# MLP up-projection of a two-layer encoder: the first k-chunk of five of eleven gate/value pairs as a seven-product unit, the gate turned at once and the gate-value product on VectorE

## The chip, the cores and the metric

The kernel runs on one core of one Trainium2 chip. The metric is device time in microseconds (us) of one execution, the median of three runs. Engines: TensorE (PE; its weight loads PEld), VectorE (DVE), ScalarE (ACT), GpSimd (POOL) and SyncE (SP), which issues the weight transfers.

## The reference

Input is x, 256 positions by 2048 features in float32. Two layers: grouped-query attention in the first, dilated sliding-window attention in the second, each followed by the gated MLP to which the change belongs:

```python
def conv_ffn(h, w_up, conv_w, conv_b, w_down):
    u = h @ w_up                       # 2048 -> 2 x 5632
    u = lax.conv_general_dilated(u, conv_w[:, None, :], (1,), ((1, 1),), ...) + conv_b   # depthwise, width 3
    gate, val = jnp.split(u, 2, axis=-1)
    return (jax.nn.silu(gate) * val) @ w_down

h = h + conv_ffn(rms_norm(h, ffn_norm[i]), w_up[i], conv_w[i], conv_b[i], w_down[i])
```

## The kernel before

**Products.** Every float32 product is made of three matmuls on operands split in two: `xh*wh + xh*wl + xl*wh`. A weight chunk of 512 rows by 512 columns comes in two `raw` tiles of 128 x 1024. ScalarE rounds `raw` to `wh` (line 139), VectorE forms `wl = raw - wh` (line 140); of each there are four buffers (`NHL`), and each pair (`wh`, `wl`) feeds 12 matmuls of 128 x 512. `feed` does one chunk (k-chunk `kg`, four k-tiles, two position blocks m): 24 matmuls for one column block. Both calls are recorded AHEAD of their place by a priority, so they stand early on their engines' queues. A scheduler lays the rest out in each engine's queue; every engine runs its queue in order.

**The seven-product unit.** `fast_unit` (lines 159 to 184) takes one k-chunk for two column blocks and does the 2 x 2 block product (two position blocks, two halves of the chunk, two column blocks) with seven products instead of eight: four sums of weight quarters on VectorE (line 173), seven pairs `wh`/`wl` (lines 174, 175), each feeding 6 matmuls: 42 for what two feeds do in 48. It needs sums of the left operand as well (`combined`), and four more PSUM sums (q = 1, 5, 6, 7), which `fold` adds to the others at the end. Before the change it is used in the down-projection and in one output projection only. There the weight sums go to three spare tiles.

**The MLP** (`ffn`). Up-projection: eleven pairs p of a gate block and a value block of 512 columns, p = 0 to 5 (half 0), then the down-projection over these, then p = 6 to 10 (half 1) and the rest of the down-projection. Per block four feeds. When a block's sums are complete they are evacuated with the norm's scale (`stg`, ScalarE), turned position-wise (`turned`: two VectorE transposes, 16 POOL copies into a tile `u`, of which three rotate), convolved (`conv`: ScalarE's centre tap and bias, VectorE's two outer taps, four 256-wide pieces each), silu on the gate `cg`, the product `cv = cg * cv`, and split into the left operands of the down-projection (`act_split`; for k-chunks 1 and 2 `combined`). These steps are Python generators: `start` queues one, and `step`, called between the matmuls of the feeds, advances the first in the list, so their place among the matmuls comes from the number of yields. `gate_gen` of pair p also does `product` of pair p-1; `value_gen` of pair p also does the convolution of its own gate and the split of pair p-1. Before the change the product of a pair is done on POOL, except for the last of each half, and the gate's turn waits for it (`issue_after`).

**Around.** `bias_lines` (lines 1118 to 1139) prepares bias lines of layer 1 beside the up-projection of layer 0. Its transfer of `oc` and its cast `oh` on POOL use slots of the operand store, tiles a0 to a11 (`pair_slot(kt)` is tile kt/2). In layer 0 a0 to a7 hold the operands of the attention output projection until it ends. The last 512 columns of the MLP's input are transposed late (`late_transpose`, n = 3): seven POOL copies `wide` (line 374), then `xh`, while p = 0 already runs over k-chunks 0 to 2.

Of the kernel before, what the change touches and what calls it, by code (L numbers as in the profile page):

```python
# [1 line left out]

# [11 lines left out]
P = 128  # L14
# [16 lines left out]
def tile_encoder(ctx: ExitStack, tc: tile.TileContext, x, xT, w_a, w_ao, q_gain, k_gain, w_b, w_bo,  # L31
# [25 lines left out]
    def nm(s):  # L57
        uid[0] += 1
        return f"{s}_{uid[0]}"
# [92 lines left out]
    def project(w, n, lhs, kgs, by_m=False):  # L152
        accs = new_acc()
        for i, kg in enumerate(kgs):
            end = i == len(kgs) - 1
            feed(accs, lhs, kg, w[n, kg], i == 0, end, by_m and end)
        return accs

    def fast_unit(acc, pick, wap0, wap1, begun, end, spot):
        def load(wap, i):  # L160
            r = raw_tile()
            nc.sync.dma_start(r.rearrange("p a c -> p (a c)"), wap[:, i * 1024:(i + 1) * 1024])
            return r

        b11, b21, b22, b12 = load(wap0, 0), load(wap0, 1), load(wap1, 1), load(wap1, 0)
        t1, t2, t4 = (spot(i) for i in range(3))
        sums = {3: (t1, b11, b12), 5: (b12, b12, b22), 7: (t2, t1, b22), 6: (t4, t2, b21)}
        for i, (q, r) in enumerate(((1, b11), (2, b21), (3, b22), (5, t1), (7, b12), (6, t2), (4, t4))):
            wh = spool.tile([P, 2, 512], F32R, tag="wh", name=nm("wh"), bufs=NHL)
            wl = spool.tile([P, 2, 512], F32R, tag="wl", name=nm("wl"), bufs=NHL)  # L170
            with tc.high_priority(offset=AHEAD):
                if q in sums:
                    nc.vector.tensor_tensor(*sums[q], ALU.add)
                nc.scalar.activation(wh, r, AF.Copy)  # L174
                nc.vector.tensor_tensor(wl, r, wh.bitcast(F32), ALU.subtract)  # L175
            xh, xl = pick[q]
            for j in range(2):
                st = q not in begun and j == 0
                sp = q in end and j == 1
                nc.tensor.matmul(acc[q], xh[:, j], wh[:, j], start=st, stop=False)  # L180
                nc.tensor.matmul(acc[q], xh[:, j], wl[:, j], start=False, stop=False)  # L181
                nc.tensor.matmul(acc[q], xl[:, j], wh[:, j], start=False, stop=sp)  # L182
            begun.add(q)
            step(i % 2 == 0)

# [299 lines left out]
    def ffn(l, hT, ss_in, cw, g_next, last, side=None):  # L485
        with tc.tile_pool(name=nm("fpool"), bufs=1) as fp:
# [82 lines left out]
            def product(value, eng=nc.gpsimd):  # L569
                n, u, cv, cg, made, _, _ = value  # L570
                yield from conv((n, u, cv))
                made.append(eng.tensor_tensor(cv, cg, cv, ALU.mult).ins)  # L572
# [12 lines left out]

            def act_split(value):
                slots, k0 = value[5:]
                cv = value[2]
                if k0 // 4 in fast:
                    slots[-1 - k0 // 4], *parts = combined(cv, k0)  # L590
                    if hf == 1:
                        plain_too(k0, 20 + 2 * fast.index(k0 // 4), *parts)
                    ready.add(k0 // 4)
                    yield
                    return
                for j in range(4):
                    hi, lo = slots[k0 + j]
                    tc.keep_in_program_order(nc.scalar.activation(hi, cv[:, j, :], AF.Copy))
                    nc.vector.tensor_tensor(lo, cv[:, j, :], hi.bitcast(F32), ALU.subtract)
                    if j == 1:  # L600
                        yield
                ready.add(k0 // 4)
# [25 lines left out]

            def flush(value):
                yield  # L630
                yield from product(value, nc.vector)
                ready.add("u")
                yield
                yield
                yield from act_split(value)

            def next_u():
                us.append(us.pop(0))
                return us[0]

            kgs = list(range(4))
            ready = set()
            for hf, (p0, p1) in enumerate(HALVES):
# [4 lines left out]
                last_value = None  # L648
                for p in range(p0, p1):
                    k0 = 4 * (p - p0)  # L650
                    slots.update(new_slots(range(k0, k0 + 4)))
                    cg = fp.tile([P, 4, NT], F32, tag="cg", name=nm("cg"))
                    cv = fp.tile([P, 4, NT], F32, tag="cv", name=nm("cv"))
                    gate, value = (p, next_u(), cg), (NPAIR + p, next_u(), cv, cg, [], slots, k0)

                    def gate_done(accs, gate=gate, last_value=last_value):
                        start(gate_gen(accs, gate, last_value))

                    if p == 0:
# [84 lines left out]

                np_ = p1 - p0
                wd = w_down[l][:, p0:p1]
                extra[0] = fp, ["raw2"]
# [368 lines left out]
    scr = dpool.tile([24, 1024], F32, name="scr")  # L1116

    def bias_lines():
        oc, oh, ln = (pair_slot(kt, [P, 1024], dt, t) for kt, t, dt in ((18, "oc", F32), (20, "oh", F32R), (22, "ln", F32)))
        nc.gpsimd.dma_start(oc, onehot)  # L1120
        rb = small.tile([P, 24], F32, name="rb", bufs=1)
        nc.gpsimd.memset(rb, 0.0)
        nc.gpsimd.memset(rb[32:33, :], -1e30)
        nc.gpsimd.dma_start(rb[:32, :], rel_bias)
        nc.gpsimd.tensor_copy(oh, oc)
# [317 lines left out]
```

## Time and profile before

| | |
|---|---|
| median of three runs | 2239.16 us (2238.94 to 2239.56) |
| the profiled execution: its time, its span | 2238.11 us, 2236.3 us |
| granted clock of TensorE | 0.999 |
| weight transfers (queue q1) | 57.2% of the 16 DMA engines' span, 429.05 MB |
| pairs of half 0, layer 0 | p = 1 from about 301 to 344.6 us, then every 43.5 us |
| pairs of half 1, layer 0 | p = 6 from 645 us, p = 10 to 862.7 us |

A row of a group reads: line, engine, operation, output<-inputs, shapes, count | busy us, mean ns of one | idle time of the engine just before, and who ended it. A row of a timeline reads: start, length, engine, line, operation. Starts and lengths overlap a little, since an engine begins an operation while the one before drains.

### The profile page before, as it was taken

The numbers are of one execution on the slowest core, as the hardware profiler recorded it, in microseconds if no ns is written. First come the engines' busy times: TensorE is split into PE (matmuls) and PEld (weight loads), VectorE is DVE, ScalarE is ACT, GpSimd is POOL, SyncE is SP. The second block draws the span as 40 slices with busy tenths as digits, with TensorE's granted clock in tenths as the row PEclk, the third lists the DMA queues.
The fourth block names the chain that finished last, engine by engine and source line by source line (L and its number), as shares of the span: only waits on it lengthen the run. The fifth ranks groups of instructions, "written<-read, shape, count | busy, mean of one in ns | idle before, by whom it ended". The sixth has DMA issues, their size and how long they took to land.

```text
span 2236.3 us, 28736 instructions
## 1 busy us (share of the span) xinstructions
PE 2221.9 (99%) x10005; PEld 1842.6 (82%) x10005; DVE 1720.0 (77%) x2211; ACT 1321.5 (59%) x1858; POOL 782.3 (35%) x1035
## 2 busy tenths in 40 slices
PE   9999999999999999999999999999999999999998
PEld 7888888888888888888888888888888888888887
DVE  6877667778876787968886878587777798677787
ACT  7676655666455666665454556566665655465664
POOL 2343255752006563040053006003756500256611
PEclk9999999999999999999999999999999999999999
DMA  8565656555665565565556555556556555655653
GB/s 303 193 217 183 220 184 200 192 191 191 203 207 194 192 196 191 197 189 197 189 185 200 177 192 173 200 183 216 194 183 205 184 199 199 210 193 187 217 194 142
DMA packets 126178, 439.58 MB, mean 197 GB/s; under 512 B 14408, under 2 KB 18248, under 8 KB 126032
## 3 DMA queue, kind: packets, MB, share of 16 engines
q1 hardware_dynamic: 123056, 429.05, 57.2%
q0 software_dynamic: 2688, 8.39, 1.5%
q8 instruction: 78, 1.28, 0.2%
q14 instruction: 68, 0.56, 0.1%
q10 hardware_dynamic: 288, 0.30, 0.0%
HBM read 432.34 MB, written 5.34 MB: 196 GB/s over the span
## 4 chain that ended last, share of the span: by engine, by line
PE 53%; DVE 2%; DMA 1%; POOL 1%; issue 0%; ACT 0%; POOLq 0%; DVEq 0%; ACTq 0%
PE acc L128 16%; PE acc L129 16%; PE acc L127 16%; DVE wl L140 1%; DMA raw<-in_w_b_dram 1%; PE ps L181 1%; PE ps L182 1%; PE ps L180 1%; DVE tT L379 1%; PE acc L181 0%; PE acc L182 0%; PE acc L180 0%; POOL wide L391 0%; PE ps L1286 0%; PE ps L332 0%
## 5 line engine op out<-in xcount | busy, mean ns | idle before, releaser
L140 DVE TENSOR_TENSOR wl<-raw,wh 128x1024 fp32r<-128x1024 f32 (+1 forms) x748 | 936.0, 1257 | 351.7 <-ACT wh L139 345.5
L139 ACT ACTIVATE wh<-raw 128x1024 fp32r<-128x1024 f32 (+1 forms) x748 | 783.3, 1050 | 630.5 <-PE acc L129 552.5
L128 PE MATMUL acc<-wl,xh 128*128 128x512 f32 x2176 | 848.1, 390 | 2.2 <-DVE wl L140 2.2
L127 PE MATMUL acc<-wh,xh 128*128 128x512 f32 x2176 | 848.5, 390 | 0.5 <-ACT wh L139 0.5
L129 PE MATMUL acc<-wh,xh 128*128 128x512 f32 x2176 | 846.8, 389 | 0.0
L555 POOL COPY u<-quad 32x256 f32<-32x256 f32 x672 | 480.6, 715 | 326.3 <-DVE quad L370 300.0
L128 PEld LDWEIGHTS acc<-wl,xh 128*128 128x128 f32 x2176 | 408.7, 188 | 88.3 <-DVE wl L140 5.7
L129 PEld LDWEIGHTS acc<-wh,xh 128*128 128x128 f32 x2176 | 408.5, 188 | 84.9
L127 PEld LDWEIGHTS acc<-wh,xh 128*128 128x128 f32 x2176 | 408.6, 188 | 84.5 <-ACT wh L139 1.1
L127 PE MATMUL acc<-wh,a 128*128 128x512 f32 x720 | 280.9, 390 | 0.0
L128 PE MATMUL acc<-wl,a 128*128 128x512 f32 x720 | 280.3, 389 | 0.0
L129 PE MATMUL acc<-wh,a 128*128 128x512 f32 x720 | 280.0, 389 | 0.0
L129 PEld LDWEIGHTS acc<-wh,a 128*128 128x128 f32 x720 | 135.1, 188 | 28.1 <-DVE a L321 0.2
L128 PEld LDWEIGHTS acc<-wl,a 128*128 128x128 f32 x720 | 135.2, 188 | 27.8 <-DVE wl L140 0.4
L127 PEld LDWEIGHTS acc<-wh,a 128*128 128x128 f32 x720 | 135.2, 188 | 27.7
L374 POOL COPY wide<-quad 32x256 f32<-32x256 f32 x133 | 89.6, 674 | 169.3 <-DVE quad L370 159.8
L391 POOL COPY wide<-quad 32x256 f32<-32x256 f32 x88 | 53.1, 603 | 234.6 <-DVE quad L370 167.5
L482 ACT ACTIVATE stg<-acc,rstd 128x512 f32<-128x512 f32 x122 | 82.8, 684 | 32.4 <-PE acc L129 32.4
L174 ACT ACTIVATE wh<-raw 128x1024 fp32r<-128x1024 f32 x56 | 59.5, 1063 | 66.4 <-PE acc L129 59.7
L572 POOL TENSOR_TENSOR cv<-cg,cv 128x1024 f32<-128x1024 f32 x18 | 58.2, 3231 | 105.3 <-DVE cv L542 105.3
L542 DVE SCALAR_TENSOR_TENSOR cg<-u,cw,cg 128x256 f32<-128x256 f32 x176 | 82.3, 511 | 4.5 <-ACT cg L534 4.5
L525 POOL MEMSET u<- 128x4 f32 x12 | 1.0, 106 | 241.3 <-DVE wl L175 221.0
(284 smaller groups left out, 2008.4 us busy)
## 6 DMA issues: line engine op xcount, KB each, us to landing
raw<-in_w_up_dram SPq DMA_DIRECT2D x352, 512.0 KB, 4.5
raw<-in_w_down_dram SPq DMA_DIRECT2D x176, 512.0 KB, 4.5
raw<-in_w_b_dram SPq DMA_DIRECT2D x144, 512.0 KB, 4.3
raw<-in_w_bo_dram SPq DMA_DIRECT2D x48, 512.0 KB, 4.1
raw<-in_w_a_dram SPq DMA_DIRECT2D x40, 512.0 KB, 4.7
raw<-in_w_ao_dram SPq DMA_DIRECT2D x32, 512.0 KB, 4.3
raw<-in_w_a_dram SPq DMA_DIRECT2D x16, 256.0 KB, 6.1
there<-quad POOLq DMA_DIRECT2D x6, 512.0 KB, 3.6
```

Of the source, the lines that this page charges most:

```text
L127: nc.tensor.matmul(accs[m], xh, wh[:, j, :], start=st, stop=False)
L128: nc.tensor.matmul(accs[m], xh, wl[:, j, :], start=False, stop=False)
L129: nc.tensor.matmul(accs[m], xl, wh[:, j, :], start=False, stop=sp)
L139: nc.scalar.activation(wh[:, c], r[:, c], AF.Copy)
L140: nc.vector.tensor_tensor(wl[:, c], r[:, c], wh[:, c].bitcast(F32), ALU.subtract)
L174: nc.scalar.activation(wh, r, AF.Copy)
L374: nc.gpsimd.tensor_copy(o[32 * c:32 * c + 32, :, 32 * q:32 * q + 32], quad[32 * q:32 * q + 32, c])
L391: nc.gpsimd.tensor_copy(dst, src)
L482: nc.scalar.activation(o[:, m, :], accs[m], AF.Copy, scale=rstd[:, m:m + 1])
L542: nc.vector.scalar_tensor_tensor(cj, halves(flat[:, j, o:o + NT])[:, ::-1], tap(n, j, i), cj, ALU.mult, ALU.add)
L555: nc.gpsimd.tensor_copy(o, src)
L572: made.append(eng.tensor_tensor(cv, cg, cv, ALU.mult).ins)
```

## The change

`UP` names p = 1, 4, 6, 7 and 10. For these `up_pair` replaces two `project` calls: three feeds of the gate block (k-chunks 1 to 3), the unit over k-chunk 0 for both blocks, then three feeds of the value block. The gate's sums are folded after the unit, on VectorE, the value's at the end. `sums` makes the left operands' sums once per half. The weight sums are written in place in the `raw` tiles. The product always runs on VectorE, the gate is turned before it, the silu of a gate in `UP` comes two steps later, the two extra `raw` buffers serve the up-projection too, operand slots are taken only when written, and `bias_lines` moves to slots 14, 16 and 18.

```diff
+UP = 1, 4, 6, 7, 10
+UP_ORDER = (1, 0), (2, 0), (3, 0), (0, None), (1, 1), (2, 1), (3, 1)
...
-        t1, t2, t4 = (spot(i) for i in range(3))
+        t1, t2, t4 = (b11, b22, b21) if spot is None else (spot(i) for i in range(3))
...
             def gate_gen(accs, blk, value):
                 s = evac_scaled(fp, accs, rstd, 1)
                 yield
-                if value is None:
-                    turned(s, blk[1])
-                    return
-                yield from product(value)
-                with tc.issue_after(value[4].pop()):
-                    turned(s, blk[1])
+                turned(s, blk[1])
+                if value is not None:
+                    yield
+                    yield from product(value)
...
-                made.append(eng.tensor_tensor(cv, cg, cv, ALU.mult).ins)
+                nc.vector.tensor_tensor(cv, cg, cv, ALU.mult)
...
-                for _ in range(1 if last else 4):
+                for _ in range(3 if gate[0] in UP else 1 if last else 4):
...
+            def sums(kg, at, r, st):
+                hts = [hT[4 * kg + j][:2] for j in range(4)]
+                for j, (hi, lo) in enumerate(hts):
+                    nc.vector.tensor_tensor(r[:, j], hi.bitcast(F32), lo.bitcast(F32), ALU.add)
+                    if j == 1:
+                        yield
...
+                for o, x, y in ((0, a21, a22), (2, a21, a11), (1, a11, st[:, 0]), (3, a12, st[:, 1])):
+                    nc.vector.tensor_tensor(st[:, o], x, y, ALU.subtract)
+                yield
+                own = [pair_slot(at + 2 * i, [P, 4, 2, P], F32R, "s") for i in range(2)]
+                split_in_order(*own, st)
...
+            def up_pair(p, order, gate_done):
+                (a2, a4), (a3, a8) = new_acc(), new_acc()
...
+                    if side is None:
+                        acc.update({q: ps_tile() for q in (1, 5, 6, 7)})
...
+                        fast_unit(acc, picks[kg], *(w_up[l][n, kg] for n in ns), begun, end, None)
+                    else:
...
+                        feed(sides[side], hT, kg, w_up[l][ns[side], kg], not begun.issuperset(mine),
+                             not later & {side, None}, begun=[m for m in range(2) if mine[m] in begun])
...
+                    nc.scalar.activation(a, acc[1], AF.Copy)
+                    tt(v, acc[6], a, ALU.subtract)
+                    tt(w, acc[7], v, ALU.add)
+                    tt(a2, a2, a, ALU.add)
+                    tt(a4, a4, w, ALU.subtract)
+                    gate_done((a2, a4))
+                    tt(v, acc[5], v, ALU.add)
+                    tt(w, acc[5], w, ALU.add)
+                tt(a3, a3, v, ALU.add)
+                tt(a8, a8, w, ALU.add)
+                return a3, a8
...
-                        va = project2(w_up[l], 0, NPAIR, hT, kgs, 1, gate_done)
+                        va = project2(w_up[l], 0, NPAIR, hT, kgs, 1, gate_done, None, (), [first])
+                    elif p in UP:
+                        va = up_pair(p, UP_ORDER, gate_done)
...
+                    extra[0] = fp, ["raw2"]
...
-        oc, oh, ln = (pair_slot(kt, [P, 1024], dt, t) for kt, t, dt in ((18, "oc", F32), (20, "oh", F32R), (22, "ln", F32)))
+        oc, oh, ln = (pair_slot(kt, [P, 1024], dt, t) for kt, t, dt in ((14, "oc", F32), (16, "oh", F32R), (18, "ln", F32)))
```

Three places in the engines' orders. Line numbers of the changed program are 3 or 4 higher up to line 555 and some 60 higher at the end.

First, VectorE in p = 4 of layer 0, from the split of `combined` on. Before, plain `wl` follow it:

```order
L314 TENSOR_TENSOR s_4261<-st_4255,s_4260 128x1024
L140 TENSOR_TENSOR wl_4270<-raw_4237,wh_4269 128x1024
L314 TENSOR_TENSOR sx_4262<-cv_3352,sx_4262 128x512
L314 TENSOR_TENSOR sx_4262<-cv_3352,sx_4262 128x256
L140 TENSOR_TENSOR wl_4290<-raw_4285,wh_4289 128x1024
L140 TENSOR_TENSOR wl_4306<-raw_4287,wh_4305 128x1024
```

The changed program, the same four rows and then the unit's first seven (`raw<-raw,raw` are weight sums; the last row is the `wl` of its fourth product):

```order
L318 TENSOR_TENSOR s_4292<-st_4286,s_4291 128x1024
L143 TENSOR_TENSOR wl_4301<-raw_4268,wh_4300 128x1024
L318 TENSOR_TENSOR sx_4293<-cv_3383,sx_4293 128x512
L318 TENSOR_TENSOR sx_4293<-cv_3383,sx_4293 128x256
L178 TENSOR_TENSOR wl_4329<-raw_4320,wh_4328 128x1024
L176 TENSOR_TENSOR raw_4320<-raw_4320,raw_4326 128x1024
L176 TENSOR_TENSOR raw_4326<-raw_4326,raw_4324 128x1024
L178 TENSOR_TENSOR wl_4339<-raw_4322,wh_4338 128x1024
L178 TENSOR_TENSOR wl_4349<-raw_4324,wh_4348 128x1024
L176 TENSOR_TENSOR raw_4324<-raw_4320,raw_4324 128x1024
L176 TENSOR_TENSOR raw_4322<-raw_4324,raw_4322 128x1024
L178 TENSOR_TENSOR wl_4360<-raw_4320,wh_4359 128x1024
```

The rows down to `sx` keep their place; eight operations stand between them and the fourth product.

Second, POOL where the attention output projection of layer 0 ends and the up-projection begins (names of semaphores in brackets). Before, the transfer of `oc` stands seven rows ahead of these, and the cast `oh` far ahead of the last `wide` copies:

```order
L1125 CAST oh_3504<-oc_3503 128x1024 [waits DMASW4_49,DVE_49,Pool_49]
L391 COPY wide_2206<-quad_2187 32x8x32 [waits DVE_49]
L391 COPY wide_2206<-quad_2187 32x8x32 [waits Pool_49]
L391 COPY wide_2206<-quad_2187 32x8x32 x6
L391 COPY wide_2318<-quad_2299 32x8x32 [waits DVE_49,Pool_49]
L391 COPY wide_2318<-quad_2299 32x8x32 x7
L391 COPY wide_2466<-quad_2447 32x8x32 [waits DVE_49,Activation_49,Pool_49]
L391 COPY wide_2466<-quad_2447 32x8x32 x7
L525 MEMSET u_2635 128x4 [waits PE_49,DMAHW3_49,Activation_49,Pool_49]
L525 MEMSET u_2636 128x4
L525 MEMSET u_2637 128x4
L374 COPY wide_2617<-quad_2616 32x8x32 [waits DVE_49]
```

The changed program:

```order
L395 COPY wide_2466<-quad_2447 32x8x32 x7
L1184 DMA oc_3572<-in_onehot_dram 128x1024 [waits DMASW4_49,PE_49]
L529 MEMSET u_2635 128x4 [waits DMAHW3_49,Activation_49,Pool_49]
L529 MEMSET u_2636 128x4
L529 MEMSET u_2637 128x4
L1189 CAST oh_3573<-oc_3572 128x1024 [waits DMASW4_49,DMASW6_49,DMASW2_49,DMASW0_49]
L378 COPY wide_2617<-quad_2616 32x8x32 [waits DVE_49]
```

The transfer now waits for TensorE, and the cast, which waits for the transfer, stands directly ahead of the last `wide` copies.

Third, VectorE at the end of p = 10 of layer 0. Before, from the value's transposes on:

```order
L370 STREAM_TRANSPOSE quad_7757<-stg_7732 128x16x32 x2
L542 SCALAR_TENSOR_TENSOR cg_7354<-u_5896,cw_555,cg_7354 128x256
L140 TENSOR_TENSOR wl_7836<-raw_7811,wh_7835 128x1024
L542 SCALAR_TENSOR_TENSOR cg_7354<-u_5896,cw_555,cg_7354 128x256
L599 TENSOR_TENSOR a_6970<-cv_6972,a_6970 128x256 x2
L140 TENSOR_TENSOR wl_7871<-raw_7866,wh_7870 128x1024
L599 TENSOR_TENSOR a_6969<-cv_6972,a_6969 128x256 x2
```

The changed program:

```order
L697 TENSOR_TENSOR acc_7470<-acc_7470,fold_7716 128x512
L698 TENSOR_TENSOR acc_7471<-acc_7471,fold_7716 128x512
L143 TENSOR_TENSOR wl_7963<-raw_7939,wh_7962 128x1024
L374 STREAM_TRANSPOSE quad_7894<-stg_7869 128x16x32 x2
L143 TENSOR_TENSOR wl_8006<-raw_8001,wh_8005 128x1024
L546 SCALAR_TENSOR_TENSOR cg_7466<-u_5954,cw_555,cg_7466 128x256 x8
L143 TENSOR_TENSOR wl_8022<-raw_8003,wh_8021 128x1024
L602 TENSOR_TENSOR a_7978<-cv_7086,a_7978 128x256 x2
L143 TENSOR_TENSOR wl_8052<-raw_8047,wh_8051 128x1024
L602 TENSOR_TENSOR a_7979<-cv_7086,a_7979 128x256 x2
```

Two folds stand ahead of the transposes, and all eight outer taps of the gate `cg` behind them, where two were.

More of the change, by code (lines that the diff above doesn't have):

```diff
@@ L1 @@
 from contextlib import ExitStack
+from functools import partial
 import concourse.bass as bass
@@ L586, in act_split @@
             def act_split(value):
-                slots, k0 = value[5:]
+                slots, k0 = value[4:]
                 cv = value[2]
@@ L595, in act_split @@
                     return
+                slots.update(new_slots(range(k0, k0 + 4)))
                 for j in range(4):
@@ L630, in flush @@
                 yield
-                yield from product(value, nc.vector)
+                yield from product(value)
                 ready.add("u")
@@ new lines, in up_pair @@
+            def up_pair(p, order, gate_done):
+                (a2, a4), (a3, a8) = new_acc(), new_acc()
+                acc, begun = {2: a2, 3: a3, 4: a4, 8: a8}, set()
+                sides, ns = ((a2, a4), (a3, a8)), (p, NPAIR + p)
+                tt = nc.vector.tensor_tensor
+                for i, (kg, side) in enumerate(order):
+                    later = {s for _, s in order[i + 1:]}
+                    if side is None:
+                        acc.update({q: ps_tile() for q in (1, 5, 6, 7)})
+                        end = [q for q, s in ((1, None), (5, None), (6, None), (7, None), (2, 0), (4, 0), (3, 1))
+                               if not later & {None, s}]
+                        fast_unit(acc, picks[kg], *(w_up[l][n, kg] for n in ns), begun, end, None)
+                    else:
+                        mine = ((2, 4), (3, 8))[side]
+                        feed(sides[side], hT, kg, w_up[l][ns[side], kg], not begun.issuperset(mine),
+                             not later & {side, None}, begun=[m for m in range(2) if mine[m] in begun])
+                        begun.update(mine)
+                    if 0 in begun or not begun >= {1, 2} or later & {0, None}:
+                        continue
+                    begun.add(0)
+                    a, t = junk(), fp.tile([P, 2, 512], F32, tag="st", name=nm("fold"))
+                    v, w = t[:, 0], t[:, 1]
+                    nc.scalar.activation(a, acc[1], AF.Copy)
[9 more added lines that the diff above has]
+                return a3, a8
@@ L650, in ffn @@
                     k0 = 4 * (p - p0)
-                    slots.update(new_slots(range(k0, k0 + 4)))
                     cg = fp.tile([P, 4, NT], F32, tag="cg", name=nm("cg"))
                     cv = fp.tile([P, 4, NT], F32, tag="cv", name=nm("cv"))
-                    gate, value = (p, next_u(), cg), (NPAIR + p, next_u(), cv, cg, [], slots, k0)
+                    gate, value = (p, next_u(), cg), (NPAIR + p, next_u(), cv, cg, slots, k0)
                     def gate_done(accs, gate=gate, last_value=last_value):
                         start(gate_gen(accs, gate, last_value))
+                    first = partial(sums, 0, (20, 16)[hf], cg, cv)
+                    if p == p0 and hf == 1:
+                        start(first())
                     if p == 0:
-                        va = project2(w_up[l], 0, NPAIR, hT, kgs, 1, gate_done)
+                        va = project2(w_up[l], 0, NPAIR, hT, kgs, 1, gate_done, None, (), [first])
+                    elif p in UP:
+                        va = up_pair(p, UP_ORDER, gate_done)
                     else:
@@ L746, in ffn @@
                 wd = w_down[l][:, p0:p1]
-                extra[0] = fp, ["raw2"]
                 if last and hf == 1:
```

21 lines of the change are left out of this document (16 added, 5 removed).

## The prediction

> **What bounds the kernel now.** I read the page's busy shares and its chain first, then its two costliest helper lines, then what TensorE itself waits for.
>
> ```profile
> span 2236.3 us, 28736 instructions
> PE 2221.9 (99%) x10005; PEld 1842.6 (82%) x10005; DVE 1720.0 (77%) x2211; ACT 1321.5 (59%) x1858; POOL 782.3 (35%) x1035
> PE 53%; DVE 2%; DMA 1%; POOL 1%; issue 0%; ACT 0%; POOLq 0%; DVEq 0%; ACTq 0%
> L140 DVE TENSOR_TENSOR wl<-raw,wh 128x1024 fp32r<-128x1024 f32 (+1 forms) x748 | 936.0, 1257 | 351.7 <-ACT wh L139 345.5
> L139 ACT ACTIVATE wh<-raw 128x1024 fp32r<-128x1024 f32 (+1 forms) x748 | 783.3, 1050 | 630.5 <-PE acc L129 552.5
> ```
>
> TensorE is busy all the way. ScalarE's `wh` waits 552.5 us in sum for matmuls, since its buffers are not free; VectorE's `wl` then waits for `wh`. So the splitting runs ahead of TensorE as far as its four buffers let it. TensorE's own waits and its pace:
>
> ```profile
> PE ps L336 <- DVE qTl L321: 2.3, 2, 2.0
> PE acc L128 <- DVE wl L140: 2.2, 6, 0.6
> 410.88 1.37 ACT L482 ACTIVATE stg<-acc,rstd 128x512 f32<-128x512 f32 x2 [0.98 <-PE acc L129]
> 454.40 1.37 ACT L482 ACTIVATE stg<-acc,rstd 128x512 f32<-128x512 f32 x2 [0.98 <-PE acc L129]
> ```
>
> The two evacuations follow the gate sums of p=3 and p=4, each 0.98 us behind its last matmul, and between them stand the 192 matmuls of a pair: 43.52 / 192 = 0.2267 us each. Up-projection runs at that pace without a hole. The Trainium skill's "TensorE: Matmul & The Clock Gate" (section "Wait — 56ns, not 53.3ns?") gives 215.7 ns start to start for 512 columns; by it 60 matmuls would be an estimated 12.9 us. The trace disagrees by 11 ns each, and the trace is used.
>
> **The matmuls removed.** A unit does two column blocks of one k-chunk in 7 x 6 = 42 matmuls where two plain feeds take 48. Ten units (five pairs, two layers) remove 60: 60 x 0.2267 = **13.6 us**. No weight transfer is added.
>
> **What VectorE gains in work.** Rows of the same operations in the down-projection:
>
> ```profile
> L175 DVE TENSOR_TENSOR wl<-raw,wh 128x1024 fp32r<-128x1024 f32 x56 | 67.9, 1219 | 1.3 <-ACT wh L174 0.5
> L173 DVE TENSOR_TENSOR raw<-raw,raw 128x1024 f32<-128x1024 f32 x14 | 18.2, 1296 | 0.0
> L195 DVE TENSOR_TENSOR fold<-ps,fold 128x512 f32<-128x512 f32 x7 | 4.8, 689 | 0.1
> L572 DVE TENSOR_TENSOR cv<-cg,cv 128x1024 f32<-128x1024 f32 x4 | 4.9, 1225 | 0.1
> ```
>
> Per unit pair: 3 more `wl` (3.7), 4 weight sums (5.2), 8 fold operations (5.5) and the product, formerly POOL's (1.2): 15.6 us. The rows overlap a little (below, 542.83 is followed at 543.97), 0.09 us each, 16 times: **14.2 us** of VectorE's time; p=6 has no product but the end of `sums`, about the same. The pair takes TensorE 186 x 0.2267 = 42.2 us. VectorE's present load (third pair of columns) in the windows of p=1, 4, 6, 7, 10, and in half a down-projection:
>
> ```profile
> core 0: us, PE busy (x) PEld busy (x) DVE busy (x) ACT busy (x) POOL busy (x), PEclk, DMA share, GB/s
> 301.10:344.60 43.50, 43.50 (x193) 36.04 (x192) 32.80 (x41) 27.16 (x34) 32.82 (x45) 1.00 0.58 195
> 431.70:475.20 43.50, 43.50 (x194) 36.02 (x193) 32.19 (x40) 26.25 (x33) 26.76 (x33) 1.00 0.57 194
> 645.00:688.60 43.60, 43.60 (x194) 36.09 (x193) 25.65 (x26) 18.26 (x19) 10.28 (x16) 1.00 0.63 209
> 688.60:732.10 43.50, 43.50 (x193) 36.04 (x192) 31.70 (x41) 26.42 (x34) 25.19 (x33) 1.00 0.58 193
> 819.10:862.70 43.60, 43.60 (x194) 36.08 (x194) 32.56 (x42) 27.16 (x37) 26.75 (x33) 1.00 0.59 193
> 518.70:582.00 63.30, 63.30 (x280) 52.06 (x279) 57.27 (x66) 42.12 (x55) 4.53 (x8) 1.00 0.56 187
> ```
>
> With 14.2 added, VectorE needs 47.0, 46.4, 39.9, 45.9 and 46.8 us in pairs of 42.2: too much by 4.8, 4.2, none, 3.7 and 4.6. Plain pairs leave over 10 us, so a backlog ends with each; the question is whether the lead covers it. A buffer of `wl` feeds 12 matmuls, 2.72 us, so a freed one is needed again 3 x 2.72 = 8.16 us later, and `wh` (1.05) and `wl` (1.26) fill it: the lead is some 5.7 us. It covers 4.8, barely. The down-projection row bears it out: VectorE 90% busy around two such units, and TensorE has no hole.
>
> Inside a unit the lead is thinner, since a buffer lasts 6 matmuls, 1.36 us. The rows that VectorE runs now where the unit of p=4 will stand, and the unit of the down-projection:
>
> ```profile
> 439.25 1.23 DVE L314 TENSOR_TENSOR s<-st,s 128x1024 fp32r<-128x1024 f32 x1 [0.74 <-ACT s L313]
> 443.07 1.41 DVE L140 TENSOR_TENSOR wl<-raw,wh 128x1024 fp32r<-128x1024 f32 x1
> 540.56 1.21 DVE L173 TENSOR_TENSOR u<-raw,raw 128x1024 f32<-128x1024 f32 x1
> 542.83 1.22 DVE L173 TENSOR_TENSOR raw<-raw,raw 128x1024 f32<-128x1024 f32 x1
> 543.97 1.22 DVE L173 TENSOR_TENSOR u<-u,raw 128x1024 f32<-128x1024 f32 x1
> 554.10 5.30 DVE L140 TENSOR_TENSOR wl<-raw,wh 128x1024 fp32r<-128x1024 f32 x4
> ```
>
> The eleven operations of the old unit took 13.5 us (540.56 to 554.10) beside 9.5 us of matmuls, hidden. In p=4, though, `combined` of an earlier pair (`s`, `sx`) ends just ahead. TensorE ends p=3 about 1 us before the evacuation at 432.64, so the unit begins 72 matmuls later, at about 447.9. The rows up to 443.07 stay; behind it come `wl`, two sums, two `wl`, two sums and the `wl` of the fourth product: 8 x 1.14 = 9.1, or 9.7 while POOL copies. It is ready at 452.2 to 452.8 and wanted at 447.9 + 3 x 1.36 + 0.23 = 452.2: 0 to 0.6 late, I take 0.4. In p=10 `combined` also splits `c` (0.6 on VectorE and 0.4 on ScalarE ahead of it): 1.0. p=1, 6 and 7 have no `combined` there: 0. Two layers: **+2.8 us** (0 to 6, each unit late by 0.6).
>
> **The bias lines, layer 0.** `oc` moves to slots whose last reader is the attention output projection, and its transfer and cast now stand on POOL's queue ahead of the seven `wide` copies.
>
> ```profile
> 257.82 0.39 PE L129 MATMUL acc<-wh,a 128*128 128x512 f32 x1
> oc<-in_onehot_dram POOLq DMA_DIRECT2D x1, 512.0 KB, 7.2
> 200.00 1.91 POOL L1125 CAST oh<-oc 128x1024 fp32r<-128x1024 f32 x1 [4.20 <-issue]
> 262.07 3.96 POOL L374 COPY wide<-quad 32x256 f32<-32x256 f32 x7 [1.11 <-DVE tot L446]
> 266.07 1.71 ACT L324 ACTIVATE xh<-wide,gain 128x256 fp32r<-128x256 f32 x4 [0.34 <-POOL wide L374]
> 268.77 1.23 DVE L140 TENSOR_TENSOR wl<-raw,wh 128x1024 fp32r<-128x1024 f32 x1
> ```
>
> The projection's last matmul ends at 258.2; landing at 265.4, cast 267.3, copies 271.3, `xh` 273.1, `wh` 274.1 and `wl`, behind the four `xh` of VectorE, at 275.5. That `wl` is the seventh of p=0, wanted at 258.05 + 6 x 2.72 + 0.23 = 274.6. TensorE waits **+0.9 us** (0 if the transfer takes 5 us, 3 if it queues). `xh` itself and the scale are wanted only after 290.
>
> **The end of p=10.** Its value sums are now folded, then evacuated; the silu of its gate comes two steps later; and k-chunk 4 of the down-projection wants the result four feeds (21.8 us) after the pair.
>
> ```profile
> 862.66 1.37 ACT L482 ACTIVATE stg<-acc,rstd 128x512 f32<-128x512 f32 x2 [0.17 <-PE acc L129]
> 878.77 1.22 DVE L572 TENSOR_TENSOR cv<-cg,cv 128x1024 f32<-128x1024 f32 x1
> 881.04 1.09 DVE L599 TENSOR_TENSOR a<-cv,a 128x256 fp32r<-128x256 f32 x3
> ```
>
> Now the first `a` is out 18.7 us after the pair, 3 us in time. The folds add 1.2 and their evacuation waits for them; six more taps of `cg` (2.4) stand ahead of `cv`: the chain is 2 to 4 us longer. I take 0.3 per layer, **+0.6 us** (0 to 3).
>
> **Hidden.** The gate's turn at once takes POOL's 3.2 us product out of its way and is wanted later. `sums` lies in p=0 and in the down-projection, where VectorE has room. The value sums' folds (1.2 us) stand ahead of a `wl` wanted 8 us later. ScalarE gains 3 `wh` and a copy, 3.9 us, at 26 to 27 of 43. If VectorE's lead were gone, these would cost their full time.
>
> **Sum.** -13.6 + 2.8 + 0.9 + 0.6 = -9.3. The profiled execution took 2238.11 around its 2236.3 span, 1.05 below the median 2239.16; so 2228.8 for it, and **2229.9 us** beside the median.
>
> **The rivals.**
> - *Nothing is late.* All is hidden: 2239.16 - 13.6 = 2225.6. For it: the old units. Against: `combined` just ahead of two of five units.
> - *POOL's copies slow VectorE.* Rows of the same `wl`, in p=0 with POOL idle and in p=3 with it 27.8 us busy:
>
> ```profile
> L140 DVE TENSOR_TENSOR wl<-raw,wh 128x1024 fp32r<-128x1024 f32 x10 | 12.3, 1226 | 13.7 <-ACT wh L139 13.7
> L140 DVE TENSOR_TENSOR wl<-raw,wh 128x1024 fp32r<-128x1024 f32 x16 | 21.1, 1326 | 7.0 <-ACT wh L139 7.0
> ```
>
> 0.1 us each, on the 8 added two-input operations and on the 16 `wl` already there, whose lead no longer hides it: some 0.8 us per unit pair, eight of them, +6 to +8: 2236 to 2238, no change. "SBUF — State Buffer" of the Trainium skill (section "🔬 SBUF: two separate sides") says that a VectorE operation with two inputs in SBUF and a GpSimd one that reads it lock each other out for a whole instruction. By it a colliding operation would lose up to a copy (an estimate of 3.96 / 7 = 0.57 us from the row of 262.07), and this rival would cost several times as much. The trace agrees in direction only: a tenth of a microsecond.
> - *VectorE becomes the bound, slower than before.* If waits between engines eat the 5.7 us lead, the excess of each unit pair falls on TensorE: (4.8 + 4.2 + 3.7 + 4.6) x 2 = 34.6; 2225.6 + 34.6 = 2260. It decides from 1.36 us per unit pair on. Against: TensorE's full row beside 90%.
> - *The change does less than it says.* The order has exactly 60 matmuls fewer; I give it nothing.
>
> **How the numbers follow.** Forecast 0.52 (2226.5 to 2233.5), nothing late 0.20, POOL's copies 0.18, VectorE the bound 0.10. What this kernel's measurement can tell is about 0.2%, 4.5 us: faster means below 2234.7. That takes the first two, and half of the third where only some pairs suffer: 0.81; the same 0.10; slower 0.09. The range reaches from just below 2225.6 to 2237.5.
>
> **What would show it.** PE instructions 60 fewer at 0.2267 us; VectorE 46 to 47 us in p=4 and p=10 where those windows shrink to 42.2; TensorE waiting for `wl` only in these units, and once near 274 us, with POOL's cast at about 265. Waits for `wl` in p=1 and 7, or over 1.4 us in each unit, would prove me wrong.

## The result, and the profile after

The changed kernel takes **2251.84 us** in the median (2247.33 to 2254.36, four runs), against 2239.05 for the kernel before, run beside it. The ratio is 1.0059, with a 95% interval of 1.0046 to 1.0071: **0.6% slower**. The forecast was 2229.9, in a range of 2225.0 to 2237.5, with a chance of 0.09 for slower.

The page of the changed kernel, its span and busy times, and VectorE's costliest helper line:

```profile
span 2248.3 us, 28923 instructions
PE 2217.8 (99%) x9945; PEld 1833.1 (82%) x9945; DVE 1905.6 (85%) x2415; ACT 1351.5 (60%) x1902; POOL 761.5 (34%) x1017
L143 DVE TENSOR_TENSOR wl<-raw,wh 128x1024 fp32r<-128x1024 f32 (+1 forms) x708 | 887.1, 1264 | 192.6 <-ACT wh L142 187.7
```

The 60 matmuls are gone (10005 to 9945). VectorE is busy for 1905.6 us instead of 1720.0, and its idle time ahead of `wl` has fallen from 351.7 to 192.6 us: the lead over TensorE has shrunk. A share of 99% for TensorE hides the rest; its waits show it (two that stood there before, at lines 340 and 446, are left out):

```profile
PE ps L185 <- DVE wl L178: 8.1, 6, 2.1
PE acc L131 <- DVE wl L143: 4.2, 7, 1.2
PE acc L185 <- DVE wl L178: 3.4, 4, 1.1
PE acc L130 <- ACT a L601: 1.6, 1, 1.6
PE acc L130 <- ACT wh L142: 1.5, 3, 0.7
```

Line 178 is the `wl` of a unit, line 601 the split of the down-projection's operand. Before, only 2.2 us stood against `wl` in all. A wait as listed leaves out the slow start behind it, so I summed, place by place, by how much the time between the starts of two matmuls exceeds 0.2267 us:

| lost in us | layer 0 | layer 1 | forecast, each layer |
|---|---|---|---|
| unit of p=1 (319 to 325 us) | 3.2 | 3.2 | 0 |
| unit of p=4 | 0.25 | 0.25 | 0.4 |
| down-projection of half 0, near 572 us | 1.4 | 1.4 | 0 |
| unit of p=7 | 1.9 | 2.3 | 0 |
| unit of p=10 | 0.6 | 0.6 | 1.0 |
| behind p=10 (877 to 894 us) | 6.1 | 4.9 | 0.3 |

That is 13.45 + 12.65 = 26.1 us, where the stages named lost 0.2 before. With -13.6 it makes +12.5; the spans differ by 2248.3 - 2236.3 = 12.0. The unit of p=6 and the bias lines (forecast +0.9) lost nothing.

**p=1.** ScalarE, VectorE and TensorE in the timeline of the changed kernel (start, length, operation, idle before and what ended it):

```profile
307.86 1.10 ACT L538 ACTIVATE cg<-u,cw 128x256 f32<-128x256 f32 x2 [3.06 <-POOL u L559]
308.49 2.11 DVE L546 SCALAR_TENSOR_TENSOR cg<-u,cw,cg 128x256 f32<-128x256 f32 x4 [2.31 <-ACT cg L538]
310.53 1.41 DVE L143 TENSOR_TENSOR wl<-raw,wh 128x1024 fp32r<-128x1024 f32 x1
311.87 2.22 DVE L546 SCALAR_TENSOR_TENSOR cg<-u,cw,cg 128x256 f32<-128x256 f32 x4
314.01 1.41 DVE L178 TENSOR_TENSOR wl<-raw,wh 128x1024 fp32r<-128x1024 f32 x1
315.46 2.64 DVE L176 TENSOR_TENSOR raw<-raw,raw 128x1024 f32<-128x1024 f32 x2
318.02 2.75 DVE L178 TENSOR_TENSOR wl<-raw,wh 128x1024 fp32r<-128x1024 f32 x2
320.81 2.56 DVE L176 TENSOR_TENSOR raw<-raw,raw 128x1024 f32<-128x1024 f32 x2
323.29 4.62 DVE L178 TENSOR_TENSOR wl<-raw,wh 128x1024 fp32r<-128x1024 f32 x4
324.56 0.50 PE L185 MATMUL ps<-wl,s 128*128 128x512 f32 x1 [2.06 <-DVE wl L178]
```

The taps of the convolution of p=0's gate (line 546) stand right ahead of the unit. They wait for GpSimd's copies, VectorE idles 2.31 us, and from 308.49 it has no hole. While GpSimd copies (to 321.0), the unit's operations start 1.28 to 1.45 us apart; in e6 below, where the copies end at 311.6, those behind them start 1.14 us apart. The fourth product's `wl` comes 2.06 us late.

**Behind p=10.** First two rows of the kernel before, where GpSimd's copies of p=10's gate are done and ScalarE's convolution has no wait, then the changed kernel at the end of layer 0's up-projection:

```profile
843.40 11.64 POOL L555 COPY u<-quad 32x256 f32<-32x256 f32 x16
858.86 2.07 ACT L534 ACTIVATE cg<-u,cw 128x256 f32<-128x256 f32 x4
```

```profile
854.17 13.12 POOL L559 COPY u<-quad 32x256 f32<-32x256 f32 x16 [15.09 <-DVE quad L374]
866.64 0.68 DVE L698 TENSOR_TENSOR acc<-acc,fold 128x512 f32<-128x512 f32 x1
867.32 1.09 ACT L538 ACTIVATE cg<-u,cw 128x256 f32<-128x256 f32 x2 [5.68 <-DVE acc L698]
868.32 1.04 ACT L142 ACTIVATE wh<-raw 128x1024 fp32r<-128x1024 f32 x1
869.40 1.23 DVE L143 TENSOR_TENSOR wl<-raw,wh 128x1024 fp32r<-128x1024 f32 x1 [2.08 <-ACT wh L142]
873.36 4.23 DVE L546 SCALAR_TENSOR_TENSOR cg<-u,cw,cg 128x256 f32<-128x256 f32 x8
877.52 1.21 DVE L143 TENSOR_TENSOR wl<-raw,wh 128x1024 fp32r<-128x1024 f32 x1
888.64 0.50 PE L130 MATMUL acc<-wh,a 128*128 128x512 f32 x1 [1.63 <-ACT a L601]
```

ScalarE stands 5.68 us idle at the first convolution step of p=10's gate, and the next `wh` is queued behind it. `wl` comes late, the one of 877.52 behind all eight taps (TensorE lost 1.5 us at 878.8), and then the operand `a`. The row names the value's fold as what ended ScalarE's wait. But GpSimd's copies of the gate end at 854.17 + 13.12 = 867.29, at the same moment: the view alone doesn't tell which it was.

### The profile page after: what moved, and what is told of

The parts are those of the page before. It is cut to its first block, busy times and chain, and to the rows that moved or that the text cites. A ratio compares the mean times of both kernels' runs of the same rounds, so it can differ in the third digit from the quotient of the medians.

```text
span 2248.3 us, 28923 instructions
## 1 busy us (share of the span) xinstructions
PE 2217.8 (99%) x9945; PEld 1833.1 (82%) x9945; DVE 1905.6 (85%) x2415; ACT 1351.5 (60%) x1902; POOL 761.5 (34%) x1017
## 3 DMA queue, kind: packets, MB, share of 16 engines
q8 instruction: 78, 1.28, 0.2%
## 4 chain that ended last, share of the span: by engine, by line
PE 46%; DVE 5%; issue 2%; DMA 1%; POOL 1%; ACT 1%; DVEq 0%; POOLq 0%; ACTq 0%
PE acc L132 13%; PE acc L130 13%; PE acc L131 13%; DVE wl L143 2%; PE ps L185 1%; PE ps L186 1%; PE ps L184 1%; DVE wl L178 1%; DMA raw<-in_w_b_dram 1%; PE acc L185 1%; PE acc L186 1%; DMA raw<-in_w_up_dram 1%; PE acc L184 1%; DVE raw L176 1%; ACT wh L142 1%
## 5 line engine op out<-in xcount | busy, mean ns | idle before, releaser
L143 DVE TENSOR_TENSOR wl<-raw,wh 128x1024 fp32r<-128x1024 f32 (+1 forms) x708 | 887.1, 1264 | 192.6 <-ACT wh L142 187.7
L142 ACT ACTIVATE wh<-raw 128x1024 fp32r<-128x1024 f32 (+1 forms) x708 | 738.9, 1048 | 505.7 <-PE acc L132 393.9
L131 PE MATMUL acc<-wl,xh 128*128 128x512 f32 x2016 | 785.6, 390 | 1.7 <-DVE wl L143 1.7
L130 PE MATMUL acc<-wh,xh 128*128 128x512 f32 x2016 | 786.3, 390 | 0.7 <-ACT wh L142 0.7
L132 PE MATMUL acc<-wh,xh 128*128 128x512 f32 x2016 | 784.5, 389 | 0.0
L559 POOL COPY u<-quad 32x256 f32<-32x256 f32 x672 | 519.4, 773 | 451.8 <-DVE quad L374 414.9
L131 PEld LDWEIGHTS acc<-wl,xh 128*128 128x128 f32 x2016 | 378.6, 188 | 80.6 <-DVE wl L143 4.1
L130 PEld LDWEIGHTS acc<-wh,xh 128*128 128x128 f32 x2016 | 378.8, 188 | 78.5 <-ACT wh L142 1.1
L132 PEld LDWEIGHTS acc<-wh,xh 128*128 128x128 f32 x2016 | 378.5, 188 | 78.8
L177 ACT ACTIVATE wh<-raw 128x1024 fp32r<-128x1024 f32 x126 | 133.2, 1060 | 115.0 <-PE acc L132 95.8
L178 DVE TENSOR_TENSOR wl<-raw,wh 128x1024 fp32r<-128x1024 f32 x126 | 154.8, 1256 | 1.5 <-ACT wh L177 0.9
L546 DVE SCALAR_TENSOR_TENSOR cv<-u,cw,cv 128x256 f32<-128x256 f32 x176 | 85.4, 532 | 0.0
```

The source lines that it names most:

```text
L130: nc.tensor.matmul(accs[m], xh, wh[:, j, :], start=st, stop=False)
L131: nc.tensor.matmul(accs[m], xh, wl[:, j, :], start=False, stop=False)
L132: nc.tensor.matmul(accs[m], xl, wh[:, j, :], start=False, stop=sp)
L142: nc.scalar.activation(wh[:, c], r[:, c], AF.Copy)
L143: nc.vector.tensor_tensor(wl[:, c], r[:, c], wh[:, c].bitcast(F32), ALU.subtract)
L546: nc.vector.scalar_tensor_tensor(cj, halves(flat[:, j, o:o + NT])[:, ::-1], tap(n, j, i), cj, ALU.mult, ALU.add)
```

## The experiments

Each run is compared with runs of the kernel before on the same chip (its medians there: 2239.36, 2239.17 and 2239.97). The expectations subtract from 2251.84, which was not taken again beside these runs. My first theory, A, was that the loss sits where GpSimd's copies of one pair run together and into the next pair's unit (p=1 behind p=0, p=7 behind p=6), and behind p=10. Rivals: B, VectorE has too much work wherever a unit stands; C, the rest of the change costs.

| run | units | median us | ratio to before, 95% |
|---|---|---|---|
| e1 | none | 2238.82 | 0.9995 (0.9986 to 1.0004) |
| e2 | 4, 6 | 2236.78 | 0.9987 (0.9978 to 0.9996) |
| e3 | 1, 4, 6, 7 | 2245.25 | 1.0026 (1.0017 to 1.0035) |
| e4 | 2, 4, 6, 8 | 2250.33 | 1.0044 (1.0032 to 1.0057) |
| e5 taps later | 1, 4, 6, 7, 10 | 2246.09 | 1.0029 (1.0018 to 1.0041) |
| e6 value copies shared | 1, 4, 6, 7, 10 | 2250.16 | 1.0048 (1.0033 to 1.0063) |
| e7 gate copies shared | 1, 4, 6, 7, 10 | 2243.26 | 1.0016 (1.0007 to 1.0026) |
| e8 no weight sums | 1, 4, 6, 7, 10 | 2235.49 | 0.9983 (0.9974 to 0.9993) |
| e9 = e5 + e7 | 1, 4, 6, 7, 10 | 2233.58 | 0.9972 (0.9963 to 0.9981) |
| e10 = e9, `sums` later | 1, 4, 6, 7, 10 | 2232.97 | 0.9967 (0.9955 to 0.9979) |
| e11 = e10, fewer units | 1, 4, 6 | 2232.93 | 0.9970 (0.9959 to 0.9981) |
| e12 = e10, fewer units | 4, 6 | 2236.32 | 0.9984 (0.9975 to 0.9993) |

### e1 to e4: which pairs cost

e1 is the change without units:

```diff
-UP = 1, 4, 6, 7, 10
+UP = ()
...
-                    if p == p0 and hf == 1:
+                    if UP and p == p0 and hf == 1:
...
-                        va = project2(w_up[l], 0, NPAIR, hT, kgs, 1, gate_done, None, (), [first])
+                        va = project2(w_up[l], 0, NPAIR, hT, kgs, 1, gate_done, None, (), [first] if UP else ())
```

> No pair is a unit pair and the sums of k-chunk 0 are not made; the gate is still turned at once, the product is on VectorE and the bias lines have their new slots. Theory A (the loss sits where GpSimd's copies run through a unit, and behind p=10): nothing is late, 2239 us, ratio 1.000 +- 0.001. Rival C (the gate's early turn and the product on VectorE cost by themselves): 3 to 10 us of the 26 us of new waits are still there, 2242 to 2249 us. Theory B (VectorE's added work is too much, wherever the unit stands, 2.6 us in each of ten unit pairs): 2239 us as A.

No change: the early turn, the product on VectorE and the bias lines cost nothing by themselves, and C falls.

e2, e3 and e4 change only the pairs:

```diff
-UP = 1, 4, 6, 7, 10
+UP = 4, 6
```

> Units in p=4 and p=6 only, the two pairs in whose units TensorE hardly waited. Theory A: 4 units x 1.36 = 5.4 us less, and the waits that the changed kernel shows for them, 0.25 in p=4 and 1.26 at 572 us in each layer: 2239.05 - 5.4 + 3.0 = 2236.6 us. Theory B: 4 x 2.6 = 10.4 us of waits, 2244 us.

Measured 2236.78: A, to the microsecond, with waits where it put them (some 0.27 in p=4 of each layer, 1.1 near 571 us and 1.3 at its like in layer 1).

> The changed kernel without the unit of p=10. Theory A: its waits of 0.48 + 6.1 (layer 0) and some 5.4 (layer 1) go, and 2.7 us of saved matmuls with them: 2251.84 - 12.0 + 2.7 = 2242.5 us. Theory B: only 2 x 2.6 us go, and 2.7 come back: 2249 us.

2245.25: 6.6 of the 9.3 us that A expected from leaving out p=10's unit. The stretch behind p=10 loses nothing now, but in this profile p=7 lost 3.9 us and p=1 4.8 us in layer 0, 2.0 and 1.6 more than in the changed kernel.

> Four units in each layer as in the run with p=1, 4, 6, 7, but each behind a plain pair whose gate and value come 21.8 us apart, so that GpSimd's copies of one pair do not run together. Theory A: 8 x 1.36 = 10.9 us less, waits of 0.25 in each unit and 1.26 near 572 us: 2239.05 - 10.9 + 4.5 = 2232.7 us, some 10 us under the run with p=1, 4, 6, 7. Theory B: the same as that run.

**A fails here**: 2250.33 and not 2232.7. TensorE's two largest waits in e4:

```profile
PE acc L131 <- DVE wl L143: 6.8, 16, 0.9
PE ps L185 <- DVE wl L178: 4.6, 2, 2.3
```

Two of them in its timeline, and ScalarE and VectorE around them:

```profile
399.49 0.50 PE L131 MATMUL acc<-wl,xh 128*128 128x512 f32 x1 [0.51 <-DVE wl L143]
413.43 0.50 PE L131 MATMUL acc<-wl,xh 128*128 128x512 f32 x1 [0.94 <-DVE wl L143]
...
394.81 1.09 ACT L538 ACTIVATE cg<-u,cw 128x256 f32<-128x256 f32 x2 [5.84 <-POOL u L559]
402.30 2.23 DVE L546 SCALAR_TENSOR_TENSOR cg<-u,cw,cg 128x256 f32<-128x256 f32 x4
406.32 1.15 DVE L612 TENSOR_TENSOR st<-cv 128x256 f32<-128x256 f32 x2
407.93 1.42 DVE L143 TENSOR_TENSOR wl<-raw,wh 128x1024 fp32r<-128x1024 f32 x1
```

The units of p=2 and p=8 lose nothing themselves. The waits are in p=3 and p=9, the plain pairs behind them, and in the unit of p=4, which loses 3.4 and 2.9 us here and 0.25 without a unit in p=2. In p=3 two things come together: ScalarE stands 5.84 us idle, to 394.81, for copies that GpSimd makes in one piece behind p=2's unit too (379.37 to 394.78), and then taps and `combined` (line 612) stand between the `wl` on VectorE. So it isn't the rhythm of A alone. Two theories were left. D: it is VectorE's burst, the work that stands within some 15 us ahead of a unit or behind it, and not the pair's total. G: ScalarE is held by GpSimd's late copies; it was first seen behind p=10, but the row of 394.81 shows it behind p=2's unit as well, so e4 doesn't separate D from G.

### e5 to e8: which work costs

e5 moves the taps of p=0's and p=6's gate behind the next pair's unit:

```diff
-                for _ in range(3 if gate[0] in UP else 1 if last else 4):
+                for _ in range(10 if last is None else 3 if gate[0] in UP else 1):
```

> All five units; the convolution of the gate of p=0 and of p=6 starts ten steps after the pair and not four or three, so that its eight taps stand behind the unit of p=1 and p=7 on VectorE and ScalarE, not ahead of it. Theory D (a burst: what matters is the work that stands right ahead of a unit, within the lead): the waits in p=1 (2.97 and 2.95) and p=7 (1.82 and 2.08) go, 2251.84 - 9.8 = 2242 us. Rival B (too much work for VectorE in the pair): they come back later in the same or the next pair, 2252 us.

2246.09, between the two. The units of p=1 and p=7 lost nothing any more (D), but in p=2, 0.9 and 1.4 us came back, and in p=8, 1.3 in each layer (B), where nothing had been lost. In p=2 ScalarE now waits 3.63 us, to 353.70, for the copies of p=1's gate, so these waits can be G's as well as B's; e9 bears on that.

e6 shares the value's copies of p=0 and p=6 with ScalarE, e7 the gate's copies of the unit pairs:

```diff
-                turned(s, blk[1], blk[0] - NPAIR in (HALVES[0][1] - 1, NPAIR - 1))
+                turned(s, blk[1], blk[0] - NPAIR in (0, 6, HALVES[0][1] - 1, NPAIR - 1))
```

> All five units; of the 16 copies of the values of p=0 and p=6, eight go to ScalarE, so GpSimd copies some 6 us less in the units of p=1 and p=7. Theory P (GpSimd's copies slow VectorE's two-input operations from 1.14 to 1.3 us and so make it late): waits in p=1 and p=7 fall by half or more, 2251.84 - 5 = 2247 us, and those operations are back near 1.14 us in the second half of the unit. Theory D: the taps still stand ahead, less than 1.5 us gained: 2250.5 to 2252 us.

2250.16: 1.7 us, inside the spread. GpSimd's copies end at 311.6 in p=1 and at 694.8 in p=7, and the units' operations behind them are back at 1.14 us from start to start. p=1's loss fell from 3.2 to 1.4 us in each layer, as P said, though in this order three of the taps also stand inside the unit and not ahead of it. p=7's rose, from 1.9 and 2.3 to 4.1 us (1.6 of it at a slow clock, see the end). So the slowing has a share in p=1, and a unit can be late without it.

```diff
-                turned(s, blk[1])
+                turned(s, blk[1], blk[0] in UP)
```

> All five units; in the unit pairs eight of the gate's 16 copies go to ScalarE. Behind p=10 ScalarE waited 5.68 us (to 867.32) and GpSimd's copies of the gate ended at 867.29. Theory G (ScalarE is held by the late copies, and wh behind it): the 6.1 + 4.9 us behind p=10 mostly go, 2251.84 - 9 = 2243 us. Theory B or D (VectorE's own backlog, its folds are late by themselves): less than 3 us gained, 2249 to 2252 us.

2243.26, as G said. The same places as above, in e7:

```profile
855.83 6.30 POOL L559 COPY u<-quad 32x256 f32<-32x256 f32 x8 [15.38 <-DVE quad L374]
864.25 1.21 DVE L574 TENSOR_TENSOR cv<-cg,cv 128x1024 f32<-128x1024 f32 x1
865.58 1.10 ACT L538 ACTIVATE cg<-u,cw 128x256 f32<-128x256 f32 x2 [2.62 <-DVE cv L574]
867.13 0.68 DVE L698 TENSOR_TENSOR acc<-acc,fold 128x512 f32<-128x512 f32 x1
```

GpSimd is done at 862.1, and ScalarE starts at 865.58, *ahead* of the fold of line 698. So the fold had never held it, though the changed kernel's row says so; the copies had. What holds it now is the product of the pair before, which reads the buffer `cg` that ScalarE is to write. Behind p=10, 1.4 us are lost in each layer instead of 6.1 and 4.9: 8.3 of the 8.6 us gained.

e8 leaves VectorE's weight sums out of these units, so that its products no longer add up to the block product and it serves for its time alone:

```diff
-                if q in sums:
+                if q in sums and spot is not None:
```

> The four weight sums of each unit in the up-projection are left out (the loaded blocks are split in their place): VectorE has 10 x 4 x 1.14 to 1.3 = 46 to 52 us less work, all else stands. If VectorE's work in and around the units is the bound (B or D), the waits in the units (2.97 + 0.25 + 1.82 + 0.48 and as much in layer 1, 11 us) go, and most of the 11 us behind p=10: 2231 to 2236 us. If GpSimd's late copies are (P, G), the units lose their waits only in part and the 11 us behind p=10 stay: 2243 to 2248 us.

2235.49. Its three largest waits:

```profile
PE acc L131 <- DVE wl L143: 3.0, 7, 0.6
PE acc L130 <- ACT a L601: 2.8, 2, 1.4
PE acc L185 <- DVE wl L178: 2.2, 2, 1.2
```

The two left in line 185 are the down-projection's, near 569 us and its like in layer 1. Every unit of the up-projection has lost its waits: 1.2 us of VectorE, four times, decide there. Behind p=10, 3.2 us remain in each layer (in layer 1 another 1.6 at a slow clock, see the end), and there ScalarE's wait of 4.72 us, to 860.62, is put down to GpSimd's copies and not to the fold: that place has a cause of its own, G. In layer 0 VectorE's work has a share in it, since the changed kernel lost 4.5 us there, the slow clock left out.

### e9 to e12: the edits together

e9 has the edits of e5 and e7.

> Both edits at once, the later convolution behind p=0 and p=6 and the gate copies shared with ScalarE, all five units. If they act on separate places (bursts ahead of the units; ScalarE held behind p=10), their gains add: 2251.84 - 5.75 - 8.58 = 2237.5 us. If VectorE's total were the bound and each only moved the wait, the sum would give much less than both: 2241 us or more.

2233.58, 4 us better than the sum of the two gains: the 5.0 us that e5 had moved into p=2 and p=8 are gone as well. So VectorE's total was not the bound there, since e7's edit leaves it as it was. GpSimd's copies were, by ScalarE's wait (1.38 us in p=2 here, and no longer for them) or by the slowing of VectorE; no run separates these two. VectorE in p=1, first the `wl` of the unit in the changed kernel (305 to 331 us), then the same group in e9, then two rows of e9's timeline:

```profile
L178 DVE TENSOR_TENSOR wl<-raw,wh 128x1024 fp32r<-128x1024 f32 x7 | 8.8, 1302 | 0.0
```

```profile
L178 DVE TENSOR_TENSOR wl<-raw,wh 128x1024 fp32r<-128x1024 f32 x7 | 9.4, 1375 | 1.5 <-ACT wh L177 1.4
```

```profile
309.57 1.35 DVE L143 TENSOR_TENSOR wl<-raw,wh 128x1024 fp32r<-128x1024 f32 x1 [1.36 <-ACT wh L142]
312.29 1.33 DVE L178 TENSOR_TENSOR wl<-raw,wh 128x1024 fp32r<-128x1024 f32 x1 [1.37 <-ACT wh L177]
```

The unit's operations are no faster in e9 (the weight sums take 1300 ns against 1284); GpSimd copies beside them as before, to 327.7. But VectorE enters the unit waiting for its input, with its lead whole, and TensorE doesn't wait.

e10 holds the sums of k-chunk 0 for the second half behind the last residual addition of the first:

```diff
+                    with tc.issue_after(lastr[0]):
+                        nc.vector.tensor_tensor(r[:, j], hi.bitcast(F32), lo.bitcast(F32), ALU.add)
```

> As the run with both edits, and the sums of k-chunk 0 for the second half (p=6 on) are kept behind the last residual addition of the first half's down-projection instead of among its second pair's first unit. If they are what makes that unit wait at 572 us (1.26 in each layer), 2.6 us less: 2235 us. If the unit waits there for its transfers whatever VectorE does, the same as without this edit.

2232.97, not to be told from e9. Near 570 us the loss fell from 1.9 and 1.7 us to 0.4 and 0.1, but 0.65 in each layer came up in p=6, where the sums now stand ahead of the unit on VectorE. e11 and e12 are e10 with `UP = 1, 4, 6` and `UP = 4, 6`.

> All three edits, units in p=1, 4 and 6 only: 6 x 1.36 = 8.2 us of matmuls less, waits of some 0.9 behind p=1 and 0.25 in p=4 in each layer: 2239.2 - 8.2 + 2.3 = 2233.3 us. If each unit costs VectorE's 2.6 us wherever it stands: 2239.2 - 8.2 + 15.6 = 2246 us.

> All three edits, units in p=4 and 6 only: 5.4 us of matmuls less and 0.25 in p=4 of each layer: 2239.2 - 5.4 + 0.5 = 2234.3 us, 2.5 us under the run with these two units and the sums among the down-projection's unit.

2232.93 and 2236.32. e11's time is as forecast, in part by luck: its waits are 0.25 in p=4 and 0.75 and 0.4 in p=6, not behind p=1. It ties with e10 on six units instead of ten: in e10, 0.5 us lost in p=8, 1.2 in p=10 and 2.7 behind it eat most of the 5.4 us that the units of p=7 and p=10 save. e12 misses its forecast by 2 us and doesn't differ from e2: the sums that lie later save 1.3 us near 570 us and cost 1.5 in p=6. e9, e10 and e11 beat both kernels, by 0.3% against before.

## Why the prediction was wrong

- **The matmuls removed, -13.6: right.** 60 are gone at 0.2267 us, and where nothing waits the saving arrives (e11: six units, 8.2 us of matmuls less, 2.0 us of waits in its profile, 7.0 us gained in the median and 6.2 between the profiled spans).
- **"p=1, 6 and 7 have no `combined` there: 0": the step that failed first.** It cost 3.2 in p=1 and about 2 in p=7, in each layer. I looked for one kind of work ahead of the unit, and another stood there already. These are rows of the kernel before:

```profile
309.06 2.10 DVE L542 SCALAR_TENSOR_TENSOR cg<-u,cw,cg 128x256 f32<-128x256 f32 x4 [2.26 <-ACT cg L534]
311.08 1.41 DVE L140 TENSOR_TENSOR wl<-raw,wh 128x1024 fp32r<-128x1024 f32 x1
312.42 2.22 DVE L542 SCALAR_TENSOR_TENSOR cg<-u,cw,cg 128x256 f32<-128x256 f32 x4
```

  Eight taps, 4.3 us, behind an idle 2.26 us, end at 314.6, and the unit's work begins in their place. e5 shows that this place is what costs; e8 shows that the unit's own extra work is the other half. The prediction named this as its own sign of being wrong: waits for `wl` in p=1 and 7.
- **"the lead is some 5.7 us. It covers 4.8, barely": the wrong account.** I set the pair's total against the lead. The windows of p=1 and p=2 in the changed kernel (VectorE is the third pair of columns):

```profile
300.30:342.90 42.60, 39.93 (x176) 32.39 (x175) 38.83 (x44) 27.92 (x33) 24.45 (x34) 1.00 0.50 180
343.00:386.00 43.00, 43.00 (x191) 35.39 (x191) 41.38 (x54) 24.76 (x33) 30.69 (x41) 1.00 0.56 189
```

  VectorE was busy for 38.8 us of p=1 and not the 47.0 that I had worked out, since part of the work fell into p=2 (41.4; before the change 32.9); TensorE waited all the same. The lead itself is 8.16 - 1.05 - 1.26 = 5.85 by its own terms, not 5.7, which changes nothing. What counts is the order within the lead's reach.
- **The end of p=10, +0.3 a layer: wrong by a factor of 15 to 20** (1.6 us of each loss is slow clock). "The chain is 2 to 4 us longer" priced VectorE's chain alone. GpSimd's copies of the gate begin at 854.17 and not at 843.40, and take 13.12 us. Of these 10.8 us, 4.1 are the 18 matmuls by which the unit makes the gate's sums later (72 + 42 stand ahead, not 96). The rest no run takes apart; the gate's folds and transposes lie in it, on a VectorE whose rows show no wait from 834.7 to 867.3. `wh` of the *next* stage (868.32) stands on ScalarE's queue behind a convolution step that waits for the copies. e7 shows it, and e3: without the unit of p=10 the place loses nothing.
- **"`sums` lies in p=0 and in the down-projection, where VectorE has room": wrong by 1.4 a layer.** In half 1 it stands among the `wl` ahead of a unit in the down-projection. Without units and sums (e1) that place loses 0.2 and 0; with the sums held back (e10) 0.4 and 0.1, but then p=6 loses 0.65.
- **p=4 and p=10 inside the unit, 0.4 and 1.0: right mechanism**, 0.25 and 0.6.
- **The bias lines, +0.9: not there.** The cast began 5.65 us after the transfer's issue instead of the 7.2 that I took, and the copies ended at 268.7, so I had the lower bound right and the value wrong:

```profile
257.76 0.62 POOL L1184 DMA_DIRECT2D oc<-in_onehot_dram  x1 [14.38 <-PE acc L132]
263.41 1.04 POOL L1189 CAST oh<-oc 128x1024 fp32r<-128x1024 f32 x1 [3.20 <-DMA oc<-in_onehot_dram]
264.40 4.30 POOL L378 COPY wide<-quad 32x256 f32<-32x256 f32 x7
```

- **Hidden: right** for the gate's turn and the product on VectorE (e1).
- **The rivals.** "VectorE becomes the bound" (2260) named the direction and the engine, but not that a unit costs nothing in p=6 and over 2 us in p=1. "POOL's copies slow VectorE" saw a true slowing, 1.14 to 1.3 us, that doesn't decide alone: in e9 it is still there and TensorE doesn't wait, in p=7 of e6 it is gone and TensorE does; in p=1 it has a share (e6). Its sum was short by its own terms, too: 0.1 us on 8 + 16 operations is 2.4 us per unit pair and not 0.8, which for eight pairs would have made 2245. By the Trainium skill's "SBUF — State Buffer" (section "🔬 SBUF: two separate sides") a collision would cost up to a whole instruction of the other engine; here it costs 0.14 to 0.25 us an operation (start to start in p=1's rows above: 2.56 / 2 and 2.79 / 2, against 1.14), and the measurement decides.

## What to carry to other kernels

Work that is added to an engine with a small lead is priced from the order of the work ahead of the place (here 16 us, 308.5 to 324.6), operation by operation, not from the stage's total: the same unit cost nothing, 0.25 or 3.2 us. No run gave the lead another size, by a fifth pair of buffers for instance. For each in-order engine ask what the delayed result's first reader has queued behind it; here the loss came from an engine at 60% whose next-stage work stood behind a wait for an engine at 34%. A releaser that ends at the same moment as another is only a suspect until one of the two is moved.

## What was not expected of the hardware

After some waits TensorE ran at about half speed. Behind p=10 in the changed kernel, the windows of its timeline (length; busy time and count of PE, PEld, DVE, ACT, POOL; granted clock; DMA share; GB/s):

```profile
886.00:890.40 4.40, 2.48 (x10) 1.46 (x9) 4.40 (x7) 2.23 (x6) 0.00 (x0) 0.99 0.47 164
890.40:894.00 3.60, 3.60 (x10) 2.79 (x10) 2.49 (x3) 1.13 (x3) 0.00 (x0) 0.54 0.69 220
894.00:898.00 4.00, 4.00 (x20) 3.27 (x19) 3.03 (x5) 2.35 (x3) 0.00 (x0) 1.00 0.65 214
```

Behind 1.9 us of idle time in 4.4 us, the granted clock was 0.54 in the next 3.6 us, and about eight matmuls in a row started 0.427 us apart, some 3.4 us together, which adds 1.6 us to the waits themselves. It isn't tied to a place: the wait of 2.06 us in p=1 had no such stretch in the changed kernel and one that cost 1.6 us in e3. The Trainium skill's "TensorE: Matmul & The Clock Gate" gives half the clock behind an idle window, in free-running windows of about 3.4 us (section "What's actually happening"), and 426.7 ns start to start for 512 columns at that clock (section "Wait — 56ns, not 53.3ns?"). Rate and length agree with the trace; the idle window doesn't, since here the stretch began behind 1.9 us of idle time in two pieces. What starts it stays open.
